# Loading the values of four heads in one transfer and spreading them on chip, in a softmax-times-values kernel

## The chip, the cores and the metric

The kernel runs on one core of one Trainium2 chip. The metric is the device time of an execution in microseconds (us); a quoted time is the median of a kernel's runs. The span of a profile, from the first to the last instruction, is some 2 us shorter than the device time of the same run.

## The reference

```python
def setup_inputs():
    batch, n_heads, seq, head_dim = 8, 12, 1024, 64
    # scores: (8, 12, 1024, 1024) fp32, v: (8, 12, 1024, 64) fp32, both randn

def reference(scores, v):
    scores_max = np.max(scores, axis=-1, keepdims=True)
    attn = np.exp(scores - scores_max)
    attn = attn / (np.sum(attn, axis=-1, keepdims=True) + 1e-8)
    return np.matmul(attn, v).astype(np.float32)
```

There are 96 heads. Each has 4 MB of scores to read, 256 KB of V to read and 256 KB of output to write: 453 MB in all, and scores are nine tenths of it.

## The kernel before

One turn of the loop takes four heads, so there are 24 turns. A head's scores lie as 128 partitions x 8 rows x 1024 keys. For each of the 8 rows ScalarE makes exp in fp16 (two rows an instruction), TensorE turns the 1024 keys of 128 queries in eight transposes (keys on partitions, `psT`), VectorE brings the result to SBUF (`pt`, the "eviction"), and eight matmuls with `vones` (V with a column of ones, which yields the row sum) add up in PSUM. After four rows VectorE divides by the sum. The subtraction of the maximum is left out, in both kernels. All loads and stores go through the sync queue in a fixed order.

```python
    v_bh = v.rearrange("b h (p c) d -> (b h) p c d", p=P)      # 2 KB runs
    # ... (cut)
    v_bufs = buffers(sb_pool, AHEAD, [P, C, D], FP32, "v_sb")  # AHEAD = 4
    out_bufs = buffers(sb_pool, 4, [P, R, D], FP32, "out_sb")
    # ... (cut)
    def finish(u):                       # one row: 8 matmuls; after 4 rows the division
        # ... (cut)
        if r == R - 1:
            dma = nc.sync.dma_start(out=one(out_bh, n), in_=st["out_sb"][:])   # 256 KB

    def load(k, n, parts=(R,), **cond):
        queue(nc.sync.dma_start(out=v_bufs[k][:], in_=one(v_bh, n), **cond))   # 256 KB
        r = 0
        for rows in parts:
            queue(nc.sync.dma_start(out=s_bufs[k][:, r : r + rows, :],
                                    in_=one(sc_bh, n)[:, r : r + rows, :], **cond))
            r += rows

    def load_last(n0):                   # third and fourth head of the next turn
        # ... (cut)
        with tc.If(n0 < BH - 2 * AHEAD) as cmp:
            loads((R,), (R,))
        with cmp.Else():
            with tc.If(n0 < BH - AHEAD):           # before the last turn: in pieces
                loads((4, 4), (2, 2, 2, 2))

    def heads(n0):
        for k in range(AHEAD):
            nc.gpsimd.tensor_copy(out=vones_bufs[k][:, :, 0:D], in_=v_bufs[k][:])
            for r in range(R):
                if r % EB == 0:          # EB = 2 rows of exp an instruction
                    # ... (cut) nc.scalar.activation(out=p_nat[...], in_=s_bufs[k][...], func=EXP)
                p_row = p_nat[:, r % EB, :].rearrange("p (q c) -> p c q", c=C)
                for c in range(C):
                    nc.tensor.transpose(out=psT[:, c * P : (c + 1) * P], in_=p_row[:, c, :],
                                        identity=ident16[:])
                nc.vector.tensor_copy(out=pt[:], in_=psT[:])
                # ... (cut) finish() follows two rows behind
        load_last(n0)
```

## Time and profile before

| | before |
|---|---|
| time, median of 3 runs | 1068.6 us (1068.58 to 1068.85) |
| span of the profile | 1066.8 us |
| DMA queue | 99.8% of 16 engines' span, 425 GB/s |
| TensorE, ScalarE, VectorE, GpSimd busy | 71%, 69%, 57%, 6% |
| granted TensorE clock, mean | 0.845 |

The DMA engines are full from end to end and everything else has a third of its time free.

### The profile page before, as it was taken

What the parts mean: (1) busy time and instruction counts of PE and PEld (TensorE: products, weight loads), DVE (VectorE), ACT (ScalarE), POOL (GpSimd) and SP (SyncE); (2) the same over time, 40 slices, a digit from 0 to 9 for tenths busy, and PEclk for the clock granted to TensorE, in tenths of its full rate; (3) what the DMA queues carried; (4) which work ended last, traced back from release to release, by engine and by line L of the source; (5) the groups of instructions that cost most, each with busy time, mean ns of one, the idle gap of its engine ahead of it and who ended that gap; (6) DMA issues with size and microseconds to landing.
All of it is one profiled execution on the core that took longest, in us unless ns stands there. A gap on an engine that the chain in (4) does not pass through costs nothing.

```text
span 1066.8 us, 32321 instructions
## 1 busy us (share of the span) xinstructions
PE 762.6 (71%) x12288; PEld 722.4 (68%) x12288; DVE 609.8 (57%) x1157; ACT 736.3 (69%) x432; POOL 59.9 (6%) x102
## 2 busy tenths in 40 slices
PE   3766767677776777668686777767776777767777
PEld 3766766677776767667676767767666677767766
DVE  2655555555564655656565565655555555555556
ACT  4757676676867768577676766677766767667686
POOL 0000000000000000000000000000000000000000
PEclk9888888878888888987888798887898788888889
DMA  9999999999999999999999999999999999999996
GB/s 402 424 425 426 432 431 421 437 434 424 429 430 435 423 440 428 430 429 420 439 430 433 424 432 435 430 423 427 436 433 424 439 422 429 428 439 429 431 423 265
DMA packets 42051, 453.05 MB, mean 425 GB/s; under 512 B 4672, under 2 KB 4672, under 8 KB 29248
## 3 DMA queue, kind: packets, MB, share of 16 engines
q1 hardware_dynamic: 42048, 453.00, 99.8%
q8 instruction: 3, 0.05, 0.0%
HBM read 436.73 MB, written 25.17 MB: 433 GB/s over the span
## 4 chain that ended last, share of the span: by engine, by line
DMA 49%; PE 20%; PEld 9%; ACT 8%; DVE 7%; issue 3%; SPq 3%; DVEq 0%; ACTq 0%
DMA s_nat<-in_scores_dram 49%; PE psT L190 13%; ACT p_nat L182 8%; PE psO L105 7%; PEld L190 6%; DVE pt L196 5%; PEld L105 3%; DVE out_sb L117 2%; SPq L140 1%; SPq L124 1%; SPq L144 1%; DVE recip L116 0%; SPq L166 0%; DVEq L196 0%; ACTq L182 0%
## 5 line engine op out<-in xcount | busy, mean ns | idle before, releaser
L182 ACT ACTIVATE p_nat<-s_nat 128x2048 f16<-128x2048 f32 (+1 forms) x408 | 705.5, 1800 | 253.5 <-DMA s_nat<-in_scores_dram 130.6
L190 PE MATMUL psT<-ident,p_nat 128*128 128x128 f16 x6144 | 583.9, 254 | 257.0 <-ACT p_nat L182 256.1
L196 DVE COPY pt<-psT 128x1024 f16<-128x1024 f16 x768 | 519.2, 690 | 429.2 <-PE L190 138.2
L190 PEld LDWEIGHTS <-p_nat 128*128 128x128 f16 x6144 | 501.3, 154 | 274.9 <-ACT p_nat L182 271.1
L105 PE MATMUL psO<-vones,pt 128*128 128x65 f16 x6144 | 375.8, 205 | 41.8 <-DVE pt L196 37.5
L105 PEld LDWEIGHTS <-pt 128*128 128x128 f16 x6144 | 309.0, 107 | 64.0 <-DVE pt L196 60.3
L175 POOL CAST vones<-v_sb 128x512 f16<-128x512 f32 x96 | 59.2, 617 | 987.7 <-PE L105 443.7
L117 DVE TENSOR_TENSOR out_sb<-psO,recip 128x256 f32<-128x256 f32 x192 | 80.8, 421 | 4.2
L182 ACT ACT_TABLE_LOAD x24 | 30.8, 1283 | 69.6 <-DMA s_nat<-in_scores_dram 64.8
L116 DVE RECIPROCAL recip<-psO 128x4 f32<-128x4 f32 x192 | 33.4, 174 | 18.0 <-PE psO L105 18.0
L57 DVE MEMSET vones<- 128x8 f16 x4 | 0.2, 65 | 0.8 <-PEq L226 0.8
L51 DVE CAST ident<-ident 128x128 f16<-128x128 f32 x1 | 0.2, 228 | 0.3 <-POOL ident masks.py:199 0.3
masks.py:199 POOL TENSOR_SCALAR_AFFINE_SELECT ident<-ident 128x128 f32<-128x128 f32 x1 | 0.3, 293 | 0.1
masks.py:197 POOL MEMSET ident<- 128x128 f32 x1 | 0.2, 204 | 0.3 <-POOLq L226 0.3
L226 POOL MEMSET const-float32-0.0<- 128x1 f32 x1 | 0.1, 98 | 0.2 <-issue 0.2
L226 POOL MEMSET const-bfloat16-1.0<- 128x1 bf16 x1 | 0.1, 101 | 0.0
L226 POOL MEMSET const-uint8-127<- 128x1 uint8 x1 | 0.1, 101 | 0.0
L226 POOL MEMSET const-float32-1.0<- 128x1 f32 x1 | 0.1, 98 | 0.0
## 6 DMA issues: line engine op xcount, KB each, us to landing
s_nat<-in_scores_dram SPq DMA_DIRECT2D x96, 4096.0 KB, 27.1
v_sb<-in_v_dram SPq DMA_DIRECT2D x98, 256.0 KB, 20.6
out_dram<-out_sb SPq DMA_DIRECT2D x96, 256.0 KB, 18.0
s_nat<-in_scores_dram SPq DMA_DIRECT2D x2, 2048.0 KB, 19.9
s_nat<-in_scores_dram SPq DMA_DIRECT2D x4, 1024.0 KB, 18.7
```

The source lines that it names most:

```text
L51: nc.vector.tensor_copy(out=ident16[:], in_=ident32[:])
L105: nc.tensor.matmul(out=psO[:, g, :], lhsT=pt[:, c * P : (c + 1) * P], rhs=st["vones"][:, c, :], start=(c == 0), stop=(c == C - 1),)
L116: nc.vector.reciprocal(out=recip[:], in_=psO[:, :, D : D + 1])
L117: nc.vector.tensor_tensor(out=st["out_sb"][:, r - G + 1 : r + 1, :], in0=psO[:, :, 0:D], in1=recip[:].to_broadcast([P, G, D]), op=mybir.Al ...
L124: dma = nc.sync.dma_start(out=one(out_bh, n), in_=st["out_sb"][:])
L140: queue(nc.sync.dma_start(out=v_bufs[k][:], in_=one(v_bh, n), **cond))
L144: nc.sync.dma_start(out=s_bufs[k][:, r : r + rows, :], in_=one(sc_bh, n)[:, r : r + rows, :], **cond,)
L175: nc.gpsimd.tensor_copy(out=vones_bufs[k][:, :, 0:D], in_=v_bufs[k][:])
L182: nc.scalar.activation(out=p_nat[:, g : g + rows, :], in_=s_bufs[k][:, r + g : r + g + rows, :], func=EXP,)
L190: nc.tensor.transpose(out=psT[:, c * P : (c + 1) * P], in_=p_row[:, c, :], identity=ident16[:],)
L196: nc.vector.tensor_copy(out=pt[:], in_=psT[:])
L226: nc = _bacc.Bacc("TRN2", target_bir_lowering=False, num_devices=1)
```

## The change

The intent is to make V's transfers cheaper. V of a head is read as 32 partitions of 8 KB runs, so that four heads fill 128 partitions and come in one 1 MB transfer a turn. One GpSimd cast makes fp16 of all four. Then VectorE spreads each head's 32 partitions over the 128 of `vones` with four copies of 32 partitions x 512. The spread puts keys in another order than before, so exp writes its output with the keys reordered in runs of eight to match. The first two heads of a turn share one store of 512 KB, which leaves 8 transfers a turn instead of 12; the last head's last two rows come in two pieces instead of one. (`vones` also gets a spare column, 66 for 65.)

```diff
-    v_bh = v.rearrange("b h (p c) d -> (b h) p c d", p=P)
+    v_bh = v.rearrange("b h (i t) d -> (b h i) (t d)", i=Q)          # Q = 32, S = 4
...
-    v_bufs = buffers(sb_pool, AHEAD, [P, C, D], FP32, "v_sb")
+    v_sb = sb_pool.tile([P, S, C, D], FP32, name="v_sb")
+    v_half = sb_pool.tile([P, S, C, D], FP16, name="v_half")
-    out_bufs = buffers(sb_pool, 4, [P, R, D], FP32, "out_sb")
+    out_pair = sb_pool.tile([P, 2, R, D], FP32, name="out_pair")
+    out_last = buffers(sb_pool, AHEAD - 2, [P, 1, R, D], FP32, "out_sb")
...
+        if r == R - 1 and k > 0:
+            if k == 1:
+                dma = nc.sync.dma_start(out=pair(out_bh, n), in_=out_pair[:])
+            else:
+                dma = nc.sync.dma_start(out=one(out_bh, n), in_=out_rows[k])
...
+    def spread_v(k):
+        for s in range(S):
+            nc.vector.tensor_copy(
+                out=vones_bufs[k][s * Q : (s + 1) * Q, :, 0:D],
+                in_=v_half[k * Q : (k + 1) * Q, s],
+            )
...
-                loads((4, 4), (2, 2, 2, 2))
+                load(AHEAD - 2, BH - 2, (4, 4))
+                load(AHEAD - 1, BH - 1, (2, 2, 2, 1, 1))
...
-            nc.gpsimd.tensor_copy(out=vones_bufs[k][:, :, 0:D], in_=v_bufs[k][:])
+            spread_v(k)
...
-                            out=p_nat[:, g : g + rows, :],
-                            in_=s_bufs[k][:, r + g : r + g + rows, :],
+                            out=p_nat[:, g : g + rows, :].rearrange("p r (s v) -> p s r v", s=S),
+                            in_=s_bufs[k][:, r + g : r + g + rows, :].rearrange(
+                                "p r (i s c) -> p s (r i) c", s=S, c=C),
```

In the order of the queue, V of the next turn's four heads comes between the scores of a turn's third and fourth head, a whole turn ahead of its use.

## The prediction

> **What bounds the kernel now.** I read the page's slices and queue table first, to see whether any unit is full all the time.
>
> ```profile
> DMA  9999999999999999999999999999999999999996
> GB/s 402 424 425 426 432 431 421 437 434 424 429 430 435 423 440 428 430 429 420 439 430 433 424 432 435 430 423 427 436 433 424 439 422 429 428 439 429 431 423 265
> DMA packets 42051, 453.05 MB, mean 425 GB/s; under 512 B 4672, under 2 KB 4672, under 8 KB 29248
> ...
> q1 hardware_dynamic: 42048, 453.00, 99.8%
> ```
>
> The 16 DMA engines are full in every slice but the last, and the one queue's packets account for 99.8% of the span. The compute engines are at 57 to 71%. So bytes and packets should set the time, provided that no engine makes the queue run dry. Only the chain of waits argues otherwise: it gives DMA 49% and the rest to engines. But a chain is one path back from the end, and where a queue is always full that path passes through compute while other transfers run. To decide it I took the rhythm of ScalarE, which starts a head's exp when its 4 MB of scores have landed:
>
> ```profile
> 475.51 7.32 ACT L182 ACTIVATE p_nat<-s_nat 128x2048 f16<-128x2048 f32 x4 [4.97 <-DMA s_nat<-in_scores_dram]
> 485.93 7.42 ACT L182 ACTIVATE p_nat<-s_nat 128x2048 f16<-128x2048 f32 x5 [3.10 <-PE L105]
> 496.14 1.28 ACT L182 ACT_TABLE_LOAD   x1 [2.79 <-DMA s_nat<-in_scores_dram]
> 497.44 7.32 ACT L182 ACTIVATE p_nat<-s_nat 128x2048 f16<-128x2048 f32 x4
> 507.12 7.32 ACT L182 ACTIVATE p_nat<-s_nat 128x2048 f16<-128x2048 f32 x4 [2.35 <-SPq L166]
> 519.39 7.32 ACT L182 ACTIVATE p_nat<-s_nat 128x2048 f16<-128x2048 f32 x4 [4.96 <-DMA s_nat<-in_scores_dram]
> ```
>
> One loop turn (four heads) goes from 475.51 to 519.39, 43.88 us. The trace's single DMA packets give the same number from below. Early in the run, where the 16 engines are still in step, the first packet of one V load to the first packet of the scores behind it is 0.646 us (eight 2 KB packets an engine, and the packet that posts the semaphore); from there to the next V load, 9.681 us (eight 32 KB packets, and one semaphore packet). A store has V's shape, so 0.646 us. Four heads: 4 x (9.681 + 0.646 + 0.646) = 43.892 us, and the semaphore packets of the trace repeat every 43.892 us through the run. Nothing but transfer time is in a turn.
>
> The queue's margin is read from the issues around one turn's end:
>
> ```profile
> 498.69 0.35 SPq L140 DMA_DIRECT2D v_sb<-in_v_dram  x1
> 499.36 0.35 SPq L144 DMA_DIRECT2D s_nat<-in_scores_dram  x1
> 500.15 0.33 SPq L140 DMA_DIRECT2D v_sb<-in_v_dram  x1
> 500.80 0.33 SPq L144 DMA_DIRECT2D s_nat<-in_scores_dram  x1
> ```
>
> These wait for the store of the turn's fourth head, so they come when compute is done with that head. The transfer then in flight, the next turn's second scores, lands at 507.12. So compute can finish about 8 us later in a turn before the DMA engines have nothing to do.
>
> **What the Trainium skill says.** "Perfetto Trace Analysis", section DMA Optimizations, says that batching small transfers into larger ones, 2 KB to 8 KB, can "dramatically improve throughput". This trace says it is little: packets of one engine start 80 ns apart at 2 KB ((646 - 6) / 8, with about 6 ns for the semaphore packet), about 1209 ns at 32 KB. That is a line of 0.03676 ns a byte plus 4.7 ns a packet, so 2 KB costs 6% of its time in overhead. "DMA: Bandwidth & Descriptors", section Why small descriptors are slow, puts it down to about 3 cycles a packet plus descriptor metadata; a fixed cost of a few ns agrees with 4.7.
>
> On exp, "Advanced Engine Details and Errata", section SBUF Cachelines, says that at least two hits on a 16-byte line are needed to hide access latency. The trace fits: the weight load that picks every eighth fp16 of p_nat (one value a line) takes 154 ns in the mean, the dense one of pt 107. The new exp reads runs of eight fp32, 32 bytes, four hits on each of two lines, so it should keep its pace of 1901 ns for 128x2048.
>
> **The change, part by part.**
>
> *V's packets.* Out: 96 loads of 8 x 2 KB packets an engine, 96 x 8 x 80 ns = 61.4 us. In: 24 loads of 1 MB, 8 x 8 KB packets an engine. No row has an 8 KB packet in the steady part; by the line above one takes 4.7 + 8192 x 0.03676 = 306 ns (estimate), so 24 x 8 x 306 = 58.8 us. Gain 2.7 us, all on the path, as the queue is never idle. The bytes do not change.
>
> *Semaphore packets.* Each transfer ends with one on each engine. Transfers: 96 V + 96 stores + 100 scores (94 whole, 2 halves, 4 quarters) = 292, and 292 x 16 = 4672, the page's count under 512 B. After: 24 + 72 + 101 = 197. 95 fewer on each engine at some 6 ns: 0.6 us. The pair store still writes 2 KB runs, since two heads are apart in memory, so it saves no more than this. DMA in sum: 3.3 us, 0.14 of a turn's 43.89.
>
> *VectorE.* It gets 16 copies a turn, 384 in all, of 32 partitions x 512 fp16. No row of before shows one. "VectorE: DVE Perf Modes", section Side-by-side, has a dense 16-bit copy at four elements a cycle after about 158 cycles: (128 + 158) / 0.96 = 0.30 us, an estimate; a partition-crossing copy may take longer. 384 x 0.30 = 115 us, raising VectorE from 609.8 to about 725 us (68%). The built order puts all 16 at the front of a turn, ahead of the first pt copy: a block of about 5 us behind the last multiply of the turn before. The first head's pt copies start some 3 us later; a head needs 8 x 0.69 + 2 x (0.42 + 0.17) = 6.7 us of VectorE of the 10.97 that its transfers take, so the backlog is gone by the second or third head, well ahead of the fourth, which decides the issue of the next loads. Off the path.
>
> *GpSimd.* 96 casts of 0.617 us become 24 of four times the size, about 2.4 us each. One runs when V has landed, in mid turn, and is wanted at the next turn. Off the path.
>
> *Queue.* 12 transfers a turn share eight semaphores now, and the sync queue waits 194 and 193 us in all for a scores transfer before V and scores issues. With 8 transfers a turn each has its own; these waits go and issues come earlier. The queue was full anyway: worth nothing.
>
> *Start.* A 1 MB V load comes ahead of the first scores in place of 256 KB, about 1.8 us. The first exp is that much later, but the queue stays full: no cost.
>
> *End.* The last four rows came as 2 + 2, now 2 + 1 + 1.
>
> ```profile
> 1054.85 1.91 ACT L182 ACTIVATE p_nat<-s_nat 128x2048 f16<-128x2048 f32 x1 [0.52 <-PE L105]
> ...
> 1057.39 2.01 ACT L182 ACTIVATE p_nat<-s_nat 128x1024 f16<-128x1024 f32 x2 [0.63 <-PE L105]
> ...
> 1061.87 0.42 DVE L117 TENSOR_TENSOR out_sb<-psO,recip 128x256 f32<-128x256 f32 x1
> ```
>
> The page puts the wait before 1057.39 down to PE, but the last 8 KB packet of scores ends at about 1056.9 there: it is the landing, and 4.9 us of compute and some 4.5 us of store and end follow it. Both last rows then go through exp in turn. With the rows apart, the first lands 8 x 155 ns = 1.24 us ahead (4 KB packets by the same line), and its exp of 1.04 us is hidden. Gain about 1.0 us.
>
> Sum: 1068.6 - 3.3 - 1.0 = 1064.3 us, 0.4% faster.
>
> **Rivals.** *ScalarE becomes the bound.* If the runs of eight slowed exp: ScalarE is busy 736.3 / 24 = 30.7 us a turn of 43.9, so exp has to slow by over 40%, past some 2.7 us a piece, to matter. At half speed a turn takes 16 x 3.8 + 1.5 = 62 us, the kernel about 1490. For it: no instruction here shows ScalarE reading in runs. Against it: the line argument above. 3%.
>
> *The copies starve the queue.* If one took 0.6 us and GpSimd's cast also held VectorE up, the block at a turn's front would be 10 us. VectorE's sum, 25.4 + 10 us, still fits in 43.9, and the fourth head is 30 us behind the block. Only a delay of over 8 us at the fourth head costs anything; then each further us costs 24 us in all. 3%.
>
> *Small packets cost more than their spacing shows.* The trace's own durations are 84.5 ns at 2 KB and 309 at 8 KB, of which neighbours overlap. Without overlap V gains 24 x 8 x (4 x 84.5 - 309) ns = 5.6 us, the semaphore packets 0.9, in all about 1061. 15%.
>
> *The end gains nothing.* Four of the 16 engines end some 2 us behind the others before; if the 4 KB pieces spread them further, the 1.0 us is lost and 1065.3 is left. 25%.
>
> **Range and chances.** Steady transfer counts bound this tightly, and runs agree within 0.3 us. The rivals that only shift sizes span 1061 to 1066; with a margin for the lag of engines and for the start, 1060.8 to 1067.0. Over 2% faster would need 21 us, more than V's whole overhead, so 1%. Over 2% slower needs one of the first two rivals: 4%.
>
> **What would show it.** Right: DMA full in all slices, exp still near 1.90 us, packets under 512 B down to 3152 and under 8 KB from 29248 to 3152 + 12288 + 256 = 15696, a turn of about 43.75 us on ScalarE, the last exp a single 128x1024 after its landing, VectorE near 725 us. Wrong: slices with DMA under 9 in mid run, exp rows well over 2 us, a turn longer than 43.9 us, or loads of the third and fourth head issued after the transfer in flight has landed.

## The result, and the profile after

The changed kernel takes 1071.82 us (median of 4 runs, 1070.83 to 1072.77); the kernel before, timed beside it, 1068.7 us (4 runs, 1068.58 to 1068.85). The ratio is 1.0029, 95% interval 1.0012 to 1.0046. A ratio is the mean time of one kernel's fast runs over that of the other's of the same rounds, so it is not quite the ratio of the medians. So the kernel became 0.3% slower where 0.4% faster was predicted. The time is within 2% of before, but 4.8 us above the upper end of the range.

The sizes of the steady part came out as predicted. From the page of the changed kernel, its DMA slices and queue:

```profile
DMA  9999999999999999999999999999999999999994
DMA packets 31443, 453.05 MB, mean 423 GB/s; under 512 B 3152, under 2 KB 3152, under 8 KB 15696
...
q1 hardware_dynamic: 31440, 453.00, 99.2%
```

Both packet counts are the predicted ones to the last packet, and DMA is full in every slice but the last, which is emptier than before (4 for 6). From its groups of instructions, shapes kept apart (busy us, mean ns, idle before and its releasers):

```profile
L217 ACT ACTIVATE p_nat<-s_nat 128x2048 f16<-128x2048 f32 x360 | 659.7, 1901 | 259.5 <-DMA s_nat<-in_scores_dram 229.4 <-SPq L196 28.6 <-PE L119 1.1
L182 DVE COPY vones<-v_half 32x512 f16<-32x512 f16 x384 | 109.4, 285 | 33.5 <-DVE out_sb L129 7.0 <-PE L229 6.8 <-POOL v_half L177 5.9
```

The exp with reordered keys still takes 1901 ns. A spreading copy takes 285 ns where 0.30 us was estimated.

The rhythm of a turn is where the first miss shows. ScalarE in mid run, third head to third head of the next turn:

```profile
476.76 7.32 ACT L217 ACTIVATE p_nat<-s_nat 128x2048 f16<-128x2048 f32 x4 [4.93 <-DMA s_nat<-in_scores_dram]
...
520.68 7.32 ACT L217 ACTIVATE p_nat<-s_nat 128x2048 f16<-128x2048 f32 x4 [4.95 <-DMA s_nat<-in_scores_dram]
```

That is 43.92 us, not the predicted 43.75, and no shorter than the 43.88 of before. ScalarE waits for the slowest of the 16 DMA engines. A transfer ends with 16 semaphore updates, one from each engine: from the first of the 16 to the first of them a turn later, the fastest engine's turn went from 43.892 to 43.785 us (mean of 20 turns), close to the prediction; the slowest one's, from the last to the last, only from 43.927 to 43.905. The engines drift apart: at the last turn one landing of scores is spread over 4.7 us between the engines, where it was 3.0 us.

The larger miss is at the end. VectorE's timeline around the start of the last turn, before:

```profile
1024.03 0.42 DVE L117 TENSOR_TENSOR out_sb<-psO,recip 128x256 f32<-128x256 f32 x1
1027.89 0.69 DVE L196 COPY pt<-psT 128x1024 f16<-128x1024 f16 x1 [3.43 <-PE L190]
```

And after, with the very last VectorE instruction:

```profile
1027.88 0.42 DVE L129 TENSOR_TENSOR out_sb<-psO,recip 128x256 f32<-128x256 f32 x1
1029.33 5.03 DVE L182 COPY vones<-v_half 32x512 f16<-32x512 f16 x16 [1.03 <-PE psT L229]
1034.39 1.89 DVE L235 COPY pt<-psT 128x1024 f16<-128x1024 f16 x3
...
1066.19 0.43 DVE L129 TENSOR_TENSOR out_sb<-psO,recip 128x256 f32<-128x256 f32 x1
```

The first row of the last turn is evicted at 1034.39 us, 6.5 us later than before, with the 5.03 us block of 16 copies right ahead of it. The work ends at 1066.62 us (1066.19 + 0.43), where before it ended at 1062.29 (1061.87 + 0.42, the prediction's last line).

ScalarE's timeline of the last turn, after, shows that the end no longer waits for the last landing:

```profile
1034.99 11.15 ACT L217 ACTIVATE p_nat<-s_nat 128x2048 f16<-128x2048 f32 x6 [1.08 <-DMA s_nat<-in_scores_dram]
1047.28 11.18 ACT L217 ACTIVATE p_nat<-s_nat 128x2048 f16<-128x2048 f32 x7 [1.13 <-PE L119]
```

The last seven exps, the two single rows among them, run without a gap from 1047.28 us. (The view puts the wait ahead of them down to TensorE, but the second half of the third head landed at 1047.18 us, just as the exp at 1034.99 follows a landing at 1034.89; so it is that landing.) Before, there was a separate start at 1057.39, just behind the last landing. After, the last landing is at 1057.02 us (before: 1057.20), and work goes on for 9.6 us after it (before: 5.1 us). The span divides as follows:

| us of span | before | predicted shift | measured shift |
|---|---|---|---|
| last landing of scores, slowest engine | 1057.20 | -3.3 | -0.2 |
| from there to the end of the last division | 5.1 | -1.0 | +4.5 |
| store and end | 4.5 | 0 | -0.4 |
| sum | 1066.8 | -4.3 | +3.9 |

The profile of the changed kernel is that of its slowest run (1072.77 us, span 1070.7 us). Two of its four runs had spans of 1068.9 and 1069.0 us, so up to 1.8 of the 3.9 us differs from run to run; the medians are 3.1 us apart. Readings below come from one profile of each kernel.

### The profile page after: what moved, and what is told of

It reads as the page before. It is cut to its first block, busy times and chain, and to the rows that moved or that the text cites. A ratio compares the mean times of both kernels' runs of the same rounds, so it can differ in the third digit from the quotient of the medians.

```text
span 1070.7 us, 32525 instructions
## 1 busy us (share of the span) xinstructions
PE 758.2 (71%) x12288; PEld 714.6 (67%) x12288; DVE 717.4 (67%) x1541; ACT 736.0 (69%) x432; POOL 48.1 (4%) x31
## 4 chain that ended last, share of the span: by engine, by line
DMA 64%; PE 12%; PEld 6%; DVE 5%; ACT 5%; SPq 4%; issue 3%; DVEq 0%; ACTq 0%; PEldq 0%
DMA s_nat<-in_scores_dram 64%; PE psT L229 8%; ACT p_nat L217 5%; PE psO L119 5%; PEld L229 4%; DVE pt L235 2%; PEld L119 2%; DVE out_sb L129 2%; SPq L158 2%; SPq L170 1%; SPq L139 1%; DVE vones L182 0%; DVE recip L128 0%; SPq L196 0%; DVEq L235 0%
## 5 line engine op out<-in xcount | busy, mean ns | idle before, releaser
L119 PEld LDWEIGHTS <-pt 128*128 128x128 f16 x6144 | 304.8, 106 | 155.9 <-DVE pt L235 154.4
L182 DVE COPY vones<-v_half 32x512 f16<-32x512 f16 x384 | 109.4, 285 | 33.5 <-DVE out_sb L129 7.0
L177 POOL CAST v_half<-v_sb 128x2048 f16<-128x2048 f32 x25 | 47.4, 1897 | 1000.5 <-DMA v_sb<-in_v_dram 956.8
L129 DVE TENSOR_TENSOR out_pair<-psO,recip 128x256 f32<-128x256 f32 x96 | 40.5, 422 | 4.3 <-SPq L196 1.9
L129 DVE TENSOR_TENSOR out_sb<-psO,recip 128x256 f32<-128x256 f32 x96 | 40.5, 422 | 2.5
```

Source lines behind the costliest of these rows:

```text
L119: nc.tensor.matmul(out=psO[:, g, :], lhsT=pt[:, c * P : (c + 1) * P], rhs=st["vones"][:, c, 0:M], start=(c == 0), stop=(c == C - 1),)
L129: nc.vector.tensor_tensor(out=out_rows[k][:, r - G + 1 : r + 1, :], in0=psO[:, :, 0:D], in1=recip[:].to_broadcast([P, G, D]), op=mybir.Alu ...
L177: nc.gpsimd.tensor_copy(out=v_half[:], in_=v_sb[:])
L182: nc.vector.tensor_copy(out=vones_bufs[k][s * Q : (s + 1) * Q, :, 0:D], in_=v_half[k * Q : (k + 1) * Q, s],)
```

## The experiments

Two theories were set against each other. **Copies:** the block of copies at the front of the last turn delays all the compute that follows, and nothing hides it there. **Transfers:** the loads themselves do not gain what was predicted, because of stretched packets, the new order of the queue, or the shared store. Each call of runs has its own times of the kernel before: 1069.17 us in the first (9 runs), 1069.01 in the second, 1069.09 in the third. The diffs are against the changed kernel, those named "before_..." against the kernel before.

**no_copies.** The copies are taken out of the loop and made once ahead of it. The result is wrong (V of the first four heads is used for all).

```diff
         for k in range(AHEAD):
-            spread_v(k)
...
     cast_v()
+    for k in range(AHEAD):
+        spread_v(k)
     load_v(AHEAD)
```

> The changed kernel with the 384 spreading copies taken out of the loop (done once ahead of it, so the result is wrong on purpose: every turn uses the first four heads' V). Transfers, cast, exp and stores stay as in the changed kernel. Theory A (the block of 16 VectorE copies at the front of a turn puts the last turn's compute behind its data, and packets of scores in flight during the block are stretched): the last multiply follows the last landing of scores by about 4 us as the prediction had it, not 9.6 us; no stretched packets at turn fronts; last landing spread of the engines stays near 3 us instead of 4.8; time about 1064 to 1066. Theory A1 (the block costs only the end, the stretched packets have another cause): about 1067, spread still near 4.8 us. Rival B (the last turn is late because its first head lands 1.7 us later and TensorE starts cold; copies do not matter): 1070 to 1072.

Measured: 1068.64 us, ratio 0.9994 (0.9981 to 1.0008). VectorE's first eviction of the last turn and its last instruction:

```profile
1029.84 0.69 DVE L234 COPY pt<-psT 128x1024 f16<-128x1024 f16 x1 [2.10 <-PE L228]
...
1062.07 0.42 DVE L129 TENSOR_TENSOR out_sb<-psO,recip 128x256 f32<-128x256 f32 x1
```

Without the copies the first eviction comes 4.55 us earlier and the work ends 4.13 us earlier. The loss against the kernel before is gone. (The time lies between the forecasts: 1.6 us above theory A1's and at least 1.4 us below rival B's.) But the predicted gain of 0.4% does not come either, so the copies are one half of the miss and the transfers the other: the last landing is still at 1057.2 us here.

**copies_twice.** Each copy is made twice.

```diff
-        for s in range(S):
+        for s in list(range(S)) * 2:
```

> The changed kernel with each spreading copy done twice in a row (32 per turn, same result). Theory A: the block is 10 us, the end is later by about 5 us, and more packets are stretched: 1076 to 1079, spread of landings above 6 us. A1: 1076 to 1077, spread as in the changed kernel. Rival B: within 1 us of the changed kernel, 1071 to 1073.

Measured: correct, 1076.92 us, ratio 1.0073 (1.0059 to 1.0087). VectorE in the last turn:

```profile
1028.97 7.22 DVE L182 COPY vones<-v_half 32x512 f16<-32x512 f16 x23 [1.03 <-PE L229]
1036.22 0.69 DVE L235 COPY pt<-psT 128x1024 f16<-128x1024 f16 x1
...
1068.01 0.42 DVE L129 TENSOR_TENSOR out_sb<-psO,recip 128x256 f32<-128x256 f32 x1
```

Here 23 of the 32 copies stand ahead of the first eviction and the others fall between later ones. The first eviction moves from 1034.39 to 1036.22 us (+1.83) and the end of the work from 1066.62 to 1068.43 (+1.81): what delays the first eviction of the last turn delays the end one for one. Were each turn delayed, 24 times that would be seen; the span grew by 1.8 us. One thing stays open: this kernel's device time lies 4.4 us above its span, where the others' lie about 2 us above, so some 2.4 us of its 5.1 us lie outside what the profile shows. So the forecast of 1076 to 1077 us was hit partly by luck: the end was to come about 5 us later, and in the profile it came 1.8 us later.

**copies_spaced.** The copies of the second to fourth head are put behind single evictions of the head before; only the first head's four stay ahead of the first eviction.

```diff
-            spread_v(k)
+            if k == 0:
+                spread_v(k)
...
-                nc.vector.tensor_copy(out=pt[:], in_=psT[:])
+                evict = nc.vector.tensor_copy(out=pt[:], in_=psT[:])
+                if k < AHEAD - 1 and r >= R - S:
+                    behind(spread_one(k + 1, r - (R - S)), evict)   # order on VectorE alone
```

> The changed kernel with the copies of heads 2 to 4 of a turn moved to behind single rows' evictions of the head before; only 4 of 16 stay at the front of the turn (1.3 us). Same number of copies, correct result. Theory A: the front block's 3.8 us mostly come back, as VectorE has 0.2 to 0.6 us idle per row in the last turn: 1067 to 1069. Theory that it is VectorE's total work in the last turn and not the block: as the changed kernel, 1071 to 1073. Rival B: as the changed kernel too.

Measured: correct, 1069.49 us, ratio 1.0001 (0.9988 to 1.0015). VectorE in the last turn:

```profile
1029.98 1.24 DVE L180 COPY vones<-v_half 32x512 f16<-32x512 f16 x4 [1.03 <-PE L241]
1031.25 1.89 DVE L247 COPY pt<-psT 128x1024 f16<-128x1024 f16 x3
```

The same 384 copies, the same work, placed elsewhere: the first eviction comes at 1031.25 us, the work ends at 1063.47, and the loss is gone (the time is 0.5 us above theory A's range and 1.5 us below the rivals'). So what cost time was not VectorE's load but the place of the block.

**copies_gpsimd.** The copies go to GpSimd.

```diff
-            nc.vector.tensor_copy(
+            nc.gpsimd.tensor_copy(
                 out=vones_bufs[k][s * Q : (s + 1) * Q, :, 0:D],
```

> The changed kernel with the 384 spreading copies on GpSimd, which is busy 48 us of 1070, in place of VectorE. Theory A1 (the block of copies ahead of VectorE's evictions costs the end): close to the run without the copies, 1068.3 to 1069.5, and the result correct if GpSimd may write other partitions than it reads. Rival (GpSimd holds VectorE up[...], or its copies are too slow for the first head): 1070 to 1073.

Measured: correct, 1069.67 us, ratio 1.0004 (0.9991 to 1.0018). From its groups of instructions:

```profile
L182 POOL COPY vones<-v_half 32x512 f16<-32x512 f16 x384 | 233.1, 607 | 270.9 <-PE psO L119 196.7 <-PE L119 52.7
```

A copy takes 607 ns there, twice VectorE's time, and still the kernel is faster than with the copies on VectorE, though 0.2 us above the range forecast: the first eviction is at 1029.60 us and the work ends at 1062.95. VectorE's first division of the last turn now shows a wait that the change brought in:

```profile
1036.97 0.42 DVE L129 TENSOR_TENSOR out_pair<-psO,recip 128x256 f32<-128x256 f32 x1 [0.34 <-DMA out_dram<-out_pair]
```

`out_pair` is a single buffer, so the first division of a turn must wait for the shared store of the turn before. With the block of copies ahead it was hidden.

**last_rows_two.** The last rows as 2 + 2 again.

```diff
-                load(AHEAD - 1, BH - 1, (2, 2, 2, 1, 1))
+                load(AHEAD - 1, BH - 1, (2, 2, 2, 2))
```

> The changed kernel with the last head's rows loaded as 2 + 2 + 2 + 2 again. The prediction's step for the end says 1.0 us slower than the changed kernel (about 1072.8). The reading of the trace after (the last turn is paced by TensorE's and VectorE's rows, about 0.96 us each, not by the landing of the last rows) says no difference: 1071 to 1072.3.

Measured: correct, 1072.64 us, ratio 1.0032 (1.0018 to 1.0046), against 1.0029 with the rows apart. The time does not decide: it lies between the forecasts of 1072.8 and of 1071 to 1072.3 us, and the intervals overlap. The trace does. The last pair's exp waits for its landing, yet its last eviction comes far behind it:

```profile
1057.08 2.01 ACT L217 ACTIVATE p_nat<-s_nat 128x1024 f16<-128x1024 f32 x2 [0.50 <-PE psT L229]
```

```profile
1063.01 0.69 DVE L235 COPY pt<-psT 128x1024 f16<-128x1024 f16 x1 [0.18 <-PE psT L229]
...
1063.97 0.69 DVE L235 COPY pt<-psT 128x1024 f16<-128x1024 f16 x1
```

These rows are ready at 1059.09 us and wait some 4 us for their turn, so when they land makes no difference here.

**before_last_rows_apart.** The kernel before with the last rows as 2 + 1 + 1, to see the piece where the end does wait for the landing.

```diff
-                loads((4, 4), (2, 2, 2, 2))
+                loads((4, 4), (2, 2, 2, 1, 1))
```

> The kernel before with one part of the change alone: the last four rows of scores land as 2 + 1 + 1 instead of 2 + 2. The prediction's step for the end: 1.0 us faster, about 1067.6. Rival (spread of the engines, or VectorE's order of work after the last landing, eats it): 1068.4 to 1069.

Measured: correct, 1081.4 us, ratio 1.0113 (1.0097 to 1.0128). This does not answer the question, and both forecasts missed. One more transfer in the queue changes which transfers share a semaphore, and the sync queue stood still behind the last piece: its issues for the last turn's heads, the stores among them, came only from 1057.75 us on, when that piece had landed at 1057.6, and the work ended at 1074.8. What the run shows is something else: the kernel before could not afford an extra piece, and the changed one, with 8 transfers a turn, can.

**stores_apart.** The shared store is made as two stores of 256 KB, one right behind the other.

```diff
-            if k == 1:
-                dma = nc.sync.dma_start(out=pair(out_bh, n), in_=out_pair[:])
-            else:
-                dma = nc.sync.dma_start(out=one(out_bh, n), in_=out_rows[k])
+            for m, j in ((n, 0), (n + 1, 1)) if k == 1 else ((n, k),):
+                dma = nc.sync.dma_start(out=one(out_bh, m), in_=out_rows[j])
```

> The changed kernel with the pair of heads stored by two transfers of 256 KB issued one behind the other in place of one of 512 KB. If the pair store is what stretches scores packets at a turn's front (2.5 us an engine in sum) and lets the engines drift apart (spread 3 to 4.7 us), then under 0.5 us of stretched packets and a spread under 3.2 us. If not, as in the changed kernel: 2 to 3 us, 4 to 5 us. In time within 1.5 us of the changed kernel either way.

Measured: correct, 1164.56 us, ratio 1.0892 (1.0875 to 1.0909), the largest effect. From the page, the DMA queue; from the waits of the sync queue (us in total, times, longest), its largest; and a line of its timeline in mid run:

```profile
q1 hardware_dynamic: 31824, 453.00, 94.7%
```

```profile
SPq L156 <- DMA s_nat<-in_scores_dram: 491.0, 25, 22.1
```

```profile
497.34 34.81 SPq L156 DMA_DIRECT2D s_nat<-in_scores_dram  x3
```

With nine transfers a turn on eight semaphores, the ninth shares one with a scores transfer that has just been put in the queue. The sync queue has to see that one land before it issues the next scores, up to 22 us a turn, and in the meantime the DMA engines run dry: they idled 5.3% of 1163.8 us or 62 us a piece, 53 more than in after, and a turn takes some 48 us. The other 40 of the 93 us are packets that took longer, 94.7% of 1163.8 us or 1102 us against 1062 in after: read one by one, those of scores after the first 70 us were stretched by 42.9 us an engine over their usual 1213 ns. Why, no run settles. The forecast, within 1.5 us of the changed kernel, missed by far, and the question it was made for, whether the shared store stretches packets, it cannot answer. In the changed kernel with its eight transfers the same kind of wait is 15.4 us in all. So "Queue: worth nothing" was right of the change, but the shared store is not ornament: it is what keeps the count at eight.

**before_pair_store.** The kernel before with the shared store alone.

```diff
-            dma = nc.sync.dma_start(out=one(out_bh, n), in_=st["out_sb"][:])
+            if k == 1:
+                dma = nc.sync.dma_start(out=pair(out_bh, n), in_=out_pair[:])
+            else:
+                dma = nc.sync.dma_start(out=one(out_bh, n), in_=out_rows[k])
```

> The kernel before with one part of the change alone: two heads share one store. If the pair store stretches packets: 2 us or more an engine in sum, spread above 4 us, and 1 to 2 us slower than before (1070 to 1071). If V's loads or the queue order do it: under 0.3 us in sum, spread near 3 us, within 0.5 us of before.

Measured: correct, 1069.6 us, ratio 1.0006 (0.999 to 1.0021). By itself the shared store neither gains nor loses; the forecasts for its packets were both missed, as the result lies between them (0.47 us stretched, in the table below). The spread between the engines grows a little (2.7 us in mid run, where before has 2.4 and after 4.1).

**v_four_2k.** V of four heads in one transfer of 1 MB, but in the old layout with runs of 2 KB: exp keeps the old order, and four GpSimd copies a turn fill `vones`. The rest is as changed.

```diff
-    v_bh = v.rearrange("b h (i t) d -> (b h i) (t d)", i=Q)
+    v_bh = v.rearrange("b h (p c) d -> (b h) p (c d)", p=P)
...
-        for s in range(S):
-            nc.vector.tensor_copy(out=vones_bufs[k][s * Q : (s + 1) * Q, :, 0:D],
-                                  in_=v_half[k * Q : (k + 1) * Q, s])
+        nc.gpsimd.tensor_copy(out=vones_bufs[k][:, :, 0:D], in_=v_half[:, k])
```

> The changed kernel with V still of four heads in one transfer of 1 MB, but in runs of 2 KB and in the old layout, so exp does not reorder and four plain GpSimd copies a turn replace the 16 of VectorE; pair store and last rows as changed. If the 8 KB packets of V make the engines drift and stretch packets: spread under 4 us at the end and under 1 us of stretched packets in sum. If the deeper queue (one V transfer, no shared semaphores) does it: 2 to 3 us and 4.5 us, as changed. The fastest engine's turn should be 43.89 - 0.02 us, as V's packets are the old ones. Time 1068.5 to 1070.5.

Measured: correct, 1070.44 us, ratio 1.0013 (1.0000 to 1.0027). Beside copies_gpsimd (1.0004), which also keeps VectorE free, the last landing is 1.5 us later (1059.17 against 1057.68), and the mean over the 16 engines 2.5 us (1057.05 against 1054.58). So on a mean engine the 8 KB runs are worth about the 2.7 us of the prediction, and at the slowest, which counts, 1.5. The order of exp and the number of GpSimd copies differ too; the two ratios' intervals overlap, and the times alone would not settle it.

**stores_short.** Every store writes one row of eight. The result is wrong.

```diff
-                dma = nc.sync.dma_start(out=pair(out_bh, n), in_=out_pair[:])
+                dma = nc.sync.dma_start(out=pair(out_bh, n)[:, :, 0:1, :], in_=out_pair[:, :, 0:1, :])
...
-                dma = nc.sync.dma_start(out=one(out_bh, n), in_=out_rows[k])
+                dma = nc.sync.dma_start(out=one(out_bh, n)[:, 0:1, :], in_=out_rows[k][:, 0:1, :])
```

> The changed kernel with each store cut to an eighth (256 B a partition and head, wrong on purpose, number and order of transfers kept). If score reads are stretched by the stores that engines ahead write meanwhile, the stretched packets go (under 0.5 us in sum) and the spread stays under 3 us; if something else at the turn's front does it, 2 to 3 us and over 4 us as in the changed kernel. Time falls by about seven eighths of the stores' 62 us in any case.

Measured: 1018.22 us, ratio 0.9526 (0.9511 to 0.954), which is what missing bytes save and says nothing by itself. The run was made for the packets, read one by one from the trace. A 32 KB packet of scores usually takes 1213 ns. In the changed kernel some 180 of them, after the first 70 us, took longer, by up to 694 ns (in no_copies by up to 1038). They come in bursts once a turn (502.7 to 505.3 us, 547.7 to 550.9 us), while the engines that are ahead already write the turn's stores. The excess, summed and divided by the 16 engines:

| kernel | excess, us an engine | spread of a late landing, us |
|---|---|---|
| before | 0.0 | 3.0 |
| before_pair_store | 0.47 | 3.9 |
| after | 2.47 | 4.7 |
| no_copies | 2.27 | 5.2 |
| copies_twice | 2.65 | 4.9 |
| v_four_2k | 2.06 | 4.9 |
| stores_short | 0.05 | 1.9 |

With short stores the stretching all but vanishes and the engines stay together. In the changed kernel 95% of the score packets of over 1250 ns overlap in time with packets of a store, of the others 12%; but only 11% of those that overlap are stretched, so overlap is not enough. The stretching does not come from the copies (2.27 without them, 2.65 with twice as many) nor from the 8 KB packets (2.06 without them). The shared store alone makes a fifth of it. What in the rest of the change makes the other part, the new order of the queue or the single V transfer, no run tells apart, and it stays open.

**gpsimd_table_early** and **before_table_early.** A try to beat both kernels. ScalarE loads its exp table at the front of each turn when the turn's first scores have landed (the lines with ACT_TABLE_LOAD in the prediction); an exp of one column ahead of it should draw the load forward, and the first two rows of a turn go through exp singly. The first variant has the copies on GpSimd as well; the second is the kernel before with these two edits.

```diff
+        nc.scalar.activation(out=first_out[:], in_=first[:], func=EXP)
         for k in range(AHEAD):
...
-                    rows = 1 if k == AHEAD - 1 and r == R - EB else EB
+                    rows = 1 if (k == AHEAD - 1 and r == R - EB) or (k == 0 and r == 0) else EB
```

> The changed kernel with the copies on GpSimd, and the last turn begun earlier: a one-column exp on a constant at each turn's front lets the table load (1.28 us) run before the turn's first scores land, and the first two rows of a turn go through exp one by one (the first is done 0.85 us sooner). If the last turn's compute, from the landing of its first head, sets the end: 1.5 to 2.1 us faster than the run with the copies on GpSimd, about 1067.6 to 1068.2, ahead of the kernel before (1068.7 to 1069.2). If the landing of the last head's rows sets it: no gain, 1069.5.

> The kernel before with the same two edits (early table load, first two rows one by one). Its last exp waits for the last landing at 1057.4 us, so if the landing sets its end, within 0.4 us of before; if the last turn's pace does, 1 to 2 us faster.

Measured: correct, 1071.36 us, ratio 1.0021 (1.0007 to 1.0034), and correct, 1073.65 us, ratio 1.0042 (1.0028 to 1.0056). Both missed: slower, not faster. ScalarE in the last turn of before_table_early:

```profile
1025.51 1.28 ACT L177 ACT_TABLE_LOAD   x1
1026.81 0.20 ACT L177 ACTIVATE first_out<-first 128x1 f32<-128x1 f32 x1
1028.41 7.41 ACT L186 ACTIVATE p_nat<-s_nat 128x1024 f16<-128x1024 f32 x5 [1.40 <-DMA s_nat<-in_scores_dram]
```

The table is there ahead of the scores, but the scores come late: the exp starts at 1028.41 us where before started it at 1024.84, and the last landing is 5.1 us later than before. With these edits on ScalarE the transfers were slower: after the first 70 us, 59% of the score packets of before_table_early took over 1213 ns, by at most 36, all through the run, where in before none did. That is 2.35 us an engine, with the engines 5.3 us apart; it is not the stretching in bursts of the table above. Why, and by which of the two edits, these runs do not settle. No correct version is faster than the kernel before beyond the intervals.

## Why the prediction was wrong, point by point

**Right.** *What bounds the steady part:* DMA is at 9 in every slice but the last. *V packets, Semaphore packets:* both counts hit. A V load takes 2.453 us from start to start of its packets early in the run, where the estimate of 306 ns a packet gives 8 x 306 + 6 = 2.454 us. *Exp:* 1901 ns, the pace forecast; whether the 16-byte lines are the reason no run tests. *VectorE:* 717.4 us for about 725; *GpSimd:* a cast of 1.897 us for 2.4. *Queue:* no gain. *The copies starve the queue,* given 3%, did not happen: in mid run the same block of 5.03 us stands at each turn's front and the turn still takes 43.9 us.

**Wrong: "Off the path" of the copies.** The step took a head's 6.7 us of VectorE against the 10.97 us of its transfers and had the backlog gone by the third head. In the last turn two things are otherwise. First, the pace is not VectorE's alone. A row goes from transposes to eviction to matmuls, and with transposes of 0.69 us and matmuls of 0.42 us a row, which overlap in part, TensorE and VectorE together do a row in 0.96 us (the distance of the evictions), 7.7 us a head; and the scores of the last turn's four heads land 9.7, 12.3 and 9.8 us apart, 31.8 us from the first to the last. 32 rows at 0.96 us take 30.7 us, which leaves about 1 us to catch up in. Second, TensorE's clock is at half for the first rows. TensorE's timeline after, and the granted clock (PEclk) in four windows:

```profile
1030.37 1.07 PE L229 MATMUL psT<-ident,p_nat 128*128 128x128 f16 x8 [0.60 <-ACT p_nat L217]
1035.14 0.62 PE L119 MATMUL psO<-vones,pt 128*128 128x65 f16 x8 [3.70 <-DVE pt L235]
1035.57 1.04 PE L229 MATMUL psT<-ident,p_nat 128*128 128x128 f16 x8
...
1041.42 0.69 PE L229 MATMUL psT<-ident,p_nat 128*128 128x128 f16 x8
```

```profile
core 0: us, PE busy (x) PEld busy (x) DVE busy (x) ACT busy (x) POOL busy (x), PEclk, DMA share, GB/s
1026.90:1030.20 3.30, 1.63 (x24) 1.38 (x24) 1.42 (x6) 3.30 (x2) 0.00 (x0) 1.00 0.92 396
1030.30:1031.40 1.10, 1.03 (x8) 0.82 (x8) 1.01 (x4) 1.10 (x2) 0.00 (x0) 0.50 1.08 451
1034.40:1037.00 2.60, 1.86 (x26) 1.86 (x27) 2.23 (x4) 2.01 (x2) 0.00 (x0) 0.50 1.08 444
1041.00:1043.00 2.00, 2.00 (x47) 2.00 (x45) 1.79 (x4) 1.88 (x2) 0.00 (x0) 1.00 0.96 410
```

The clock falls to 0.50 at 1030.23 us, ahead of the stall of 3.70 us behind the copies, and is back at 1.00 at 1040.47 us. Behind the stall four rows take 1.3 us each. The Trainium skill, "TensorE: Matmul & The Clock Gate", section Part 1: The HAM clock gate, says that the array runs at half rate after an idle window of about 3.4 us until it has been busy for about as long. This trace has the two rates, and 5.3 us from the end of the stall to full rate; but the fall came when TensorE had been busy for 1.63 of the last 3.30 us, with no gap over 1.17 us, so it did not take an idle window. The kernel before has half the clock there too, from 1026.91 to 1030.33 us; what the longer stretch costs by itself no run tells apart.

So there is nothing to catch up in: 30.7 us and 4 x 0.34 = 1.4 us for the slow rows make 32.1 us (an estimate), as long as the landings. From the first eviction of the last turn to the end of the work it was 32.2 us in after, and also in copies_twice and copies_spaced, whose first evictions lie elsewhere (1036.22 and 1031.25 us), and 31.9 in last_rows_two; it was 34.4 us in before: the kernel before had 2.2 us of slack there, and no more. After, the first eviction comes 6.5 us later, 1.7 of it because the last turn's first scores land later (1025.22 us for 1023.45) and the rest through the block of copies (4.55 us against no_copies, where the prediction had some 3). 6.5 - 2.2 = 4.3 us, and the work ended 4.33 us later, which is the same two spans over again and no test. In copies_spaced it is 3.36 - 2.2 = 1.2 us, and the work ended 1.18 us later; in no_copies the first eviction is 1.95 us later, within the slack, and the end moves by 0.2 us. The 1.7 us have a plain part: V of the last turn's four heads lies ahead of its first scores now, where only the first head's did, three times 0.646 us or 1.9 us more to transfer first.

The sign was in the profile of before. In mid run ScalarE waits 2.8 to 5.0 us for a landing in a turn's rhythm; in the last turn, its timeline before:

```profile
1034.56 7.33 ACT L182 ACTIVATE p_nat<-s_nat 128x2048 f16<-128x2048 f32 x4 [2.40 <-DMA s_nat<-in_scores_dram]
1042.07 3.72 ACT L182 ACTIVATE p_nat<-s_nat 128x2048 f16<-128x2048 f32 x2 [0.19 <-DMA s_nat<-in_scores_dram]
1046.94 7.39 ACT L182 ACTIVATE p_nat<-s_nat 128x2048 f16<-128x2048 f32 x4 [1.15 <-PE L105]
```

It waits 2.40 us for the second head's scores and 0.19 us for the third's. The wait ahead of 1046.94 is put down to TensorE, but ends 0.10 us after the rest of the third head landed (1046.84 us), so it is a landing too. ScalarE is ahead of the others, though; where they have room, VectorE's evictions show, from the first head's last to the second head's first:

```profile
1034.63 0.69 DVE L196 COPY pt<-psT 128x1024 f16<-128x1024 f16 x1
1037.27 0.69 DVE L196 COPY pt<-psT 128x1024 f16<-128x1024 f16 x1 [1.95 <-PE psO L105]
```

That is 2.64 us, where the pace is 0.96: they wait for the second head, which landed at 1034.45 us. From there to the last eviction (1060.21 us) the 23 steps take 1.00 us in the mean. So from the second head on the kernel before had hardly any room either. The prediction took only the last wait, ahead of 1057.39, for the limit, and did not look at how little room lay in front of it.

**Wrong: "End", a gain of 1.0 us.** The last exp no longer waits for its landing, so splitting the last rows is worth nothing (the trace of last_rows_two). The rival *The end gains nothing*, given 25%, had that outcome by the spread of the engines. The spread did grow, but here the end would not have waited for the landing at all.

**Mis-sized: "DMA in sum: 3.3 us".** The last landing moved by 0.2 us. What stands against the 3.3 us is packets of scores stretched by 2.47 us an engine, which the change itself brings about, through the stores of engines that run ahead. 3.3 - 2.47 = 0.8 us should be left, and the mean over the 16 engines moved by 0.2 (1054.88 to 1054.67 us). The table leaves out the first 70 us, in which score packets were stretched by 1.28 us an engine in after and 0.77 in before; with these 0.5 us, 0.3 should be left for the 0.2 measured. (In no_copies the same sum leaves 0.6 for 0.1, so it closes only roughly.) The drift also decides who gains: the fastest engine lands 1.8 us earlier (1054.17 to 1052.33), the slowest, for which everyone waits, 0.2. The prediction read the spacing of packets early in the run, "where the 16 engines are still in step", and took it for the whole run; the saving is real on an engine and is lost before it reaches the end.

The two misses do not add up one by one. With the copies out of the way a landing holds the end again, but by the traces not the last one, for in no_copies too the last seven exps run without a gap. The work ends 27.4 us after the last turn's second head has landed in no_copies (1035.11 to 1062.49 us), in copies_gpsimd and in v_four_2k, and 27.8 us after it in before; and in no_copies this landing is 0.7 us later than before, not earlier. So the copies explain the loss and the landings why there is no gain behind it. That it is the second head's landing is read from traces; no run moved it alone. The reverse, landings as early as predicted with the copies left in, was not run.

## What to carry to other kernels

Off the path in a steady turn is not off the path in the last one: for every instruction that a change puts at the front of a turn, ask separately what hides it in the final turn, by the time from that turn's first piece of work to the end against the arrival of its last data. When a queue of transfers is the limit, reckon with the slowest DMA engine rather than with the mean packet, and look whether the new order lets fast engines' writes run into slow engines' reads. Count the transfers of a turn against the semaphores that they share before adding or splitting one: one more cost 8.9% here, over half of it in idle DMA engines.

## What the Trainium skill lacked or had wrong

- "Perfetto Trace Analysis", section DMA Optimizations: "can dramatically improve throughput" from 2 KB to 8 KB does not hold here. A 2 KB packet costs 80 ns and an 8 KB one 306 (2.453 us for a load of eight, less the semaphore packet), 4% less for the same bytes, and between v_four_2k and copies_gpsimd it was 1.5 us at the last landing, 2.5 us in the mean of the engines, of some 1068.
- "TensorE: Matmul & The Clock Gate", section Part 1: The HAM clock gate, has half rate after an idle window of about 3.4 us; in the last turn of the changed kernel the clock fell to 0.50 after 3.30 us in which TensorE was busy for 1.63 us, with no gap over 1.17 us.
- No page that I read has it that reads are stretched while other DMA engines of the same core, further on in the same queue, write: 2.47 us an engine in the changed kernel, 0.05 with short stores, single 32 KB packets by up to 694 ns over 1213.
- No page that I read has a figure for what a shared completion semaphore costs at issue: one transfer over the eight of a turn made the sync queue wait 491 us and the kernel 8.9% slower, 53 of the 93 us in idle DMA engines.
- No page that I read explains why two edits on ScalarE, a table load drawn ahead of a turn's first scores and two rows of exp taken singly, go with later landings: 5.1 us at the end of before_table_early.
